# A decoder layer on one core: split weights written by converting and accumulating transfers instead of by ScalarE and VectorE

## The chip, the core and the metric

The kernel runs on one NeuronCore of a Trainium2 chip. The core has TensorE (matmul), VectorE, ScalarE, GpSimd and SyncE, each with its own instruction queue that runs strictly in order, and 16 DMA engines that all queues share. The metric is device time in microseconds (us) of one execution, median of three: 1070.07 us before the change.

## The reference

One layer over 512 tokens of width 1024, in float32: a SwiGLU block (hidden width 2816), a mixer, a second SwiGLU block, a final RMSNorm.

```
h = h + 0.5 * swiglu(rms_norm(h, ffn1_norm), ffn1_w1, ffn1_w3, ffn1_w2)
u = rms_norm(h, mix_norm)
s5_in, q, k, v, r, a_low, g_s5, g_gla = split(u @ w_in)
y_s5  = s5_mixer(s5_in, ...)      # diagonal state space scan, then a GLU
y_gla = gla_mixer(q, k, v, r, a_low, ...)   # chunked gated linear attention
h = h + (sigmoid(g_s5) * (y_s5 @ proj_s5) + sigmoid(g_gla) * (y_gla @ proj_gla)) @ w_out
h = h + 0.5 * swiglu(rms_norm(h, ffn2_norm), ffn2_w1, ffn2_w3, ffn2_w2)
out = rms_norm(h, final_norm)
```

The products need more precision than one pass of the type fp32r gives. So each weight and each activation is written as two fp32r numbers, hi (the rounded value) and lo (what the rounding lost), and each product is three matmuls: hi by hi, hi by lo, lo by hi.

## The kernel before, in words

Work is a list of units. A unit is one weight piece in HBM (128 partitions by 1024 floats, 512 KB; the pieces of ffn1_w2 have 768 or 640 columns) with the matmuls that use it. Most units have 8 k-steps of three matmuls (`mm3`, lines 228 to 230): L228 uses hi of the weights, L229 hi again with lo of the activations, L230 lo of the weights. Units are numbered here from 0 in the order of the list: 0 and 1 are the first pair (`lead1`, which loads x and its own weights in eight small pieces each, interleaved); 2 to 75 are the rest of the first SwiGLU; from 76 the mixer; from 119 `w_out`; from 127 the first six features of the second SwiGLU. Of the units from 2 to 138, 136 go through `load` and `split` in their plain form (104 of 1024 columns, 32 of 768 or 640); the exception is a small one of the mixer, `wal`. After unit 138 the second SwiGLU runs on other code (`ffn_seven`, a seven-product scheme) that fetches from SyncE into the same ring `raws`, and splits on ScalarE and VectorE.

The order is written out by hand, in the loop at lines 1720 to 1739; each engine's queue gets its instructions in just this order. At unit n the loop

- calls `load(n + 5)`: a ring slot is taken and SyncE transfers the piece into `raw`;
- emits the unit's matmuls and releases the slots of unit n - 1;
- calls `split(n + 3)`: ScalarE rounds `raw` into `hi` (L262), VectorE writes `lo = raw - hi` (L263). For a unit marked `urgent` (the last feature of each group of the first SwiGLU: units 11, 31, 49, 67) this comes after the unit's post-processing;
- emits the unit's post-processing (VectorE and ScalarE, for example the gate `silu(a) * b` and its own split);
- lets side generators emit a step: `s5_prep` (preparation of the state space tables, from unit 6 on), later `s5_main` and `gla`.

Rings: 5 slots of `raw`, 4 of `hi`, 4 of `lo`; `get()` gives one of NSLOT = 63 slots of 128x512 floats for everything else. A slot that is taken again makes its new writer wait for the last reader.

What runs on GpSimd before the change: `make_identity` at the start; the first step of `s5_prep`, emitted at unit 6 (three transfers, three memsets of 128x2048, then `wup` and the mask triangle `tri`, L450 to L465, after which VectorE makes `mask` from `tri`, L466); 64 small copies (L608) in four steps of 16, emitted at units 17, 17, 18 and 19; six small transfers (L649); eight tensor operations (L711, L714) emitted at unit 52; memsets of the attention part (L884, L920, L1060, L1077); four multiplications at the end (L1294). None of the weight transfers is on its queue: they are all on SyncE's.

Of the kernel before, what the change touches and what calls it, by code (L numbers as in the profile page):

```python
# [7 lines left out]
F32 = mybir.dt.float32  # L8
F32R = mybir.dt.float32r
I32 = mybir.dt.int32  # L10
U8 = mybir.dt.uint8
AF = mybir.ActivationFunctionType
ALU = mybir.AluOpType
PSUM = bass.MemoryType.PSUM

P = 128
# [4 lines left out]
GROUPS2 = [6, 4, 4, 4, 4]  # L21
BLOCKS = [(0, 256), (256, 384), (384, 512)]
EPS = 1e-6
NSLOT = 63
MAGIC = 12582912.0
HALVES = [slice(0, 256), slice(256, 512)]
STEPS_S5 = [[("a", 0)], [("b", 0)], [("s", 0), ("a", 1)], [], [("b", 1), ("c", 0)], [("s", 1), ("a", 2)], [],
# [45 lines left out]
def body(nc, tc, a):  # L73
    with tc.tile_pool(name="sb", bufs=1) as sb, \
            tc.tile_pool(name="ps", bufs=1, space=PSUM) as pp, \
            tc.manual_schedule():
        _body(nc, a, sb, pp)


def _body(nc, a, sb, pp):  # L80
    V, S, G, PE = nc.vector, nc.scalar, nc.gpsimd, nc.tensor

    def tt(out, x, y, op):
        V.tensor_tensor(out=out, in0=x, in1=y, op=op)  # L84
# [7 lines left out]
    def sub(out, x, y):  # L92
        tt(out, x, y, ALU.subtract)
# [10 lines left out]
    def act(out, x, f, **kw):  # L104
        S.activation(out, x, f, **kw)  # L105

    raws = Ring([sb.tile([P, 1024], F32, name=f"raw{i}") for i in range(5)])
    his = Ring([sb.tile([P, 1024], F32R, name=f"hi{i}") for i in range(4)])
    los = Ring([sb.tile([P, 1024], F32R, name=f"lo{i}") for i in range(4)])
    vec = sb.tile([P, 40], F32, name="vec")  # L110
    s5p = sb.tile([P, 64], F32, name="s5p")
# [12 lines left out]
    def get(dt=F32):  # L124
        made[0] += 1
        return sb.tile([P, T], dt, tag="g", name=f"g{made[0]}", bufs=NSLOT)

# [112 lines left out]
    def load(n):  # L240
        if n >= len(units):
            return
        u = units[n]
        if u.load is not None:
            u.load(u)
        else:
            u.raw = raws.take()
            nc.sync.dma_start(out=u.raw[:, 0:u.width], in_=u.src)

    def split(n):  # L250
        if n >= len(units):
            return
        u = units[n]
        if u.split is not None:
            u.split(u)
            if u.raw is not None:
                raws.drop(u.raw)
                u.raw = None
            return
        u.hi, u.lo = his.take(), los.take()  # L260
        w = u.width
        act(u.hi[:, 0:w], u.raw[:, 0:w], AF.Copy)  # L262
        sub(u.lo[:, 0:w], u.raw[:, 0:w], u.hi[:, 0:w].bitcast(F32))  # L263
        raws.drop(u.raw)
        u.raw = None

    def release(u):
        for ring, t in ((raws, u.raw), (his, u.hi), (los, u.lo)):
# [117 lines left out]
    def lead1(ua, ub, pa, pb):  # L386
# [10 lines left out]
        def mm():  # L397
            for u in (ua, ub):
                u.hi, u.lo = his.take(), los.take()
            pa[0], pb[0] = spps.get(), spps.get()  # L400
            part = lambda k: ((ua, ub)[k // 4], slice(k % 4 * 256, k % 4 * 256 + 256))
            for k in range(KT):
                u, c = part(k)
                nc.sync.dma_start(out=h[k], in_=a["x"][k])
                nc.sync.dma_start(out=u.raw[:, c], in_=a["w0"][k])
            for n in (2, 3, 4):
                load(n)
            st["n1"] = nrm = Norm()
            for k in range(KT):
                hi_lo_scaled(h[k], g1[:, k:k + 1], xs[k][0], xs[k][1])  # L410
                u, c = part(k)
                act(u.hi[:, c], u.raw[:, c], AF.Copy)
                sub(u.lo[:, c], u.raw[:, c], u.hi[:, c].bitcast(F32))
                for bank, o in ((pa[0], c.start), (pb[0], c.start + P)):
                    mm3(bank, u.hi[:, o:o + P], u.lo[:, o:o + P], xs[k][0], xs[k][1], k == 0, k == KT - 1)
            split(2)
            split(3)
            for k in range(KT):
                nrm.square(h[k])
                nrm.gather()  # L420
# [745 lines left out]
    for m in range(KT):  # L1166
        u = Unit(a["wout"][m], 1024, None)
# [171 lines left out]
    def seven_x(norm):  # L1339
# [35 lines left out]
        for k in range(4):  # L1375
            for kk in (k, k + 4):
                xn[kk] = get()
                stt(xn[kk], h[kk], g2[:, kk:kk + 1], b, ALU.mult, ALU.mult)
            low()
            split(xn[k][:, left], X["1"][0][k], X["1"][1][k], -1.0)  # L1380
            split(xn[k + 4][:, left], X["2"][0][k], X["2"][1][k])
            yield
# [333 lines left out]
    tasks.sort(key=lambda t: t[0])  # L1716
    fetches.sort(key=lambda t: t[0])
    load(0)
    load(1)
    for n, u in enumerate(units):  # L1720
        if n >= 2:
# [79 lines left out]
```

## Time and profile before

| | us |
|---|---|
| median of three runs | 1070.07 (1068.56 to 1070.69) |
| profiled execution, its own time | 1068.79 |
| its span, first to last instruction | 1067.1 |
| TensorE busy in the span | 1052.0 |
| VectorE busy | 718.3 |
| ScalarE busy | 437.7 |
| GpSimd busy | 69.1 |

The profiled execution's time is 1.7 us longer than its span. All times in the rows below are microseconds from the start of the span. PE is TensorE's matmuls, PEld its weight loads (which run beside the matmul before), DVE is VectorE, ACT ScalarE, POOL GpSimd, SP SyncE; POOLq and SPq are the queues of the latter two where they issue transfers. A row of the timeline gives start, duration, engine, line, operation, what is written from what, and how many such instructions are merged in it; in square brackets stands the idle time of the engine just before and what ended it. The line of an instruction is often that of a helper (L84 is any `tensor_tensor` of VectorE, L105 any activation of ScalarE). A unit's place in the trace is found by counting weight loads of L228: 8 for each unit of 1024 columns, 6 or 5 for the narrower ones.

### The profile page before, as it was taken

The page shows a single profiled execution, that of the slowest core. Times are in us where ns is not written, and L with a number is a line of the kernel's source. Part 1 is how long each engine was busy: PE and PEld are TensorE (multiplying, and loading weights), DVE is VectorE, ACT ScalarE, POOL GpSimd, SP SyncE. Part 2 cuts the span into 40 slices and gives each one's busy share as a digit, 9 for nine tenths or more (in the row PEclk, how much of TensorE's full clock was granted, in tenths as well). Part 3 has the DMA queues.
Part 4 walks back from the last instruction along what each step waited for, and adds up shares of the span by engine and source line. Part 5 has one row for each costly group of instructions (what it writes and reads, how often), then busy time and mean ns, then how long its engine had stood idle before and what let it go on. Part 6 is the DMA issues. An engine that isn't in the chain of part 4 may idle for free.

```text
span 1067.1 us, 14471 instructions
## 1 busy us (share of the span) xinstructions
PE 1052.0 (99%) x5544; PEld 905.4 (85%) x5544; DVE 718.3 (67%) x1401; ACT 437.7 (41%) x778; POOL 69.1 (6%) x121
## 2 busy tenths in 40 slices
PE   9999999999999999999999999999999999999995
PEld 7888888888888898888878888888899999999995
DVE  6688654797644555687385755557887778777866
ACT  7323254322222433553645233434443444544444
POOL 4002600100400000001000000000000000000002
PEclk9999999999999999999999999999999999999998
DMA  7323223322422332122122222222133233233222
GB/s 259 122 62 134 79 76 102 127 84 62 149 85 62 111 102 79 60 80 79 60 80 80 81 98 99 100 79 89 63 103 103 89 110 106 102 100 109 91 69 79
DMA packets 34388, 101.41 MB, mean 95 GB/s; under 512 B 4096, under 2 KB 5568, under 8 KB 34320
## 3 DMA queue, kind: packets, MB, share of 16 engines
q1 hardware_dynamic: 33408, 99.17, 28.3%
q0 software_dynamic: 480, 0.79, 0.3%
q8 instruction: 43, 0.70, 0.3%
q10 hardware_dynamic: 432, 0.54, 0.1%
q14 instruction: 25, 0.20, 0.1%
HBM read 98.19 MB, written 2.10 MB: 94 GB/s over the span
## 4 chain that ended last, share of the span: by engine, by line
PE 94%; ACT 2%; DVE 2%; DMA 1%; SPq 0%; issue 0%; DVEq 0%; ACTq 0%
PE mm L228 20%; PE mm L230 20%; PE mm L229 20%; PE mm L1529 5%; PE mm L1528 5%; PE mm L1526 5%; PE sp L228 3%; PE sp L229 3%; PE sp L230 3%; ACT g L105 1%; DVE g L84 1%; PE sp L999 1%; PE sp L1001 1%; PE sp L1000 1%; PE mm L1001 1%; PE mm L1000 1%
## 5 line engine op out<-in xcount | busy, mean ns | idle before, releaser
L228 PE MATMUL mm<-g,hi 128*128 128x512 f32 x944 | 374.2, 396 | 0.0
L230 PE MATMUL mm<-g,lo 128*128 128x512 f32 x944 | 369.6, 392 | 0.1
L229 PE MATMUL mm<-g,hi 128*128 128x512 f32 x944 | 369.3, 391 | 0.0
L84 DVE TENSOR_TENSOR lo<-raw,hi 128x1024 fp32r<-128x1024 f32 (+3 forms) x176 | 198.6, 1133 | 131.8 <-ACT hi L105 131.4
L105 ACT ACTIVATE g<-g 128x512 f32<-128x512 f32 (+4 forms) x227 | 130.5, 582 | 339.0 <-DVE g L84 327.2
L105 ACT ACTIVATE hi<-raw 128x1024 fp32r<-128x1024 f32 (+3 forms) x176 | 170.1, 974 | 110.3 <-PE mm L229 63.8
L230 PEld LDWEIGHTS mm<-g,lo 128*128 128x128 f32 x944 | 177.6, 188 | 41.1 <-DVE lo L84 0.6
L84 DVE TENSOR_TENSOR g<-g,g 128x512 fp32r<-128x512 f32 (+7 forms) x342 | 184.6, 558 | 38.6 <-ACT g L105 32.1
L229 PEld LDWEIGHTS mm<-g,hi 128*128 128x128 f32 x944 | 177.9, 188 | 37.2
L228 PEld LDWEIGHTS mm<-g,hi 128*128 128x128 f32 x944 | 177.8, 188 | 37.1
L84 DVE TENSOR_TENSOR g<-mm,g 128x512 f32<-128x512 f32 (+1 forms) x104 | 58.2, 564 | 47.3 <-PE mm L1529 17.2
L228 PE MATMUL sp<-g,g 128*128 128x512 f32 (+1 forms) x176 | 65.6, 373 | 0.0
L229 PE MATMUL sp<-g,g 128*128 128x512 f32 (+1 forms) x176 | 65.4, 372 | 0.0
L230 PE MATMUL sp<-g,g 128*128 128x512 f32 (+1 forms) x176 | 65.0, 369 | 0.0
L84 DVE TENSOR_TENSOR g<-g,mm 128x512 f32<-128x512 f32 (+1 forms) x72 | 44.3, 623 | 19.7 <-PE mm L230 15.3
L105 ACT ACTIVATE g<-mm 128x256 f32<-128x256 f32 (+1 forms) x50 | 19.3, 387 | 90.6 <-PE mm L1529 78.1
L1529 PE MATMUL mm<-b,lo 128*128 128x256 f32 x192 | 53.6, 279 | 0.0
L1529 PE MATMUL mm<-g,lo 128*128 128x256 f32 x192 | 53.6, 279 | 0.0
L1528 PE MATMUL mm<-b,hi 128*128 128x256 f32 x192 | 53.5, 279 | 0.0
L1526 PE MATMUL mm<-b,hi 128*128 128x256 f32 x192 | 53.5, 279 | 0.0
L1528 PE MATMUL mm<-g,hi 128*128 128x256 f32 x192 | 53.5, 279 | 0.0
L1526 PE MATMUL mm<-g,hi 128*128 128x256 f32 x192 | 53.5, 279 | 0.0
(176 smaller groups left out, 1260.0 us busy)
## 6 DMA issues: line engine op xcount, KB each, us to landing
raw<-win SPq DMA_DIRECT2D x24, 512.0 KB, 3.5
raw<-w1b SPq DMA_DIRECT2D x22, 512.0 KB, 3.5
raw<-w3b SPq DMA_DIRECT2D x22, 512.0 KB, 3.5
raw<-w1a SPq DMA_DIRECT2D x21, 512.0 KB, 3.5
raw<-w3a SPq DMA_DIRECT2D x21, 512.0 KB, 3.5
raw<-w2b SPq DMA_DIRECT2D x32, 256.0 KB, 2.7
raw<-w2a SPq DMA_DIRECT2D x16, 384.0 KB, 3.1
raw<-w2a SPq DMA_DIRECT2D x16, 320.0 KB, 2.8
```

The source lines that it names most:

```text
L84: V.tensor_tensor(out=out, in0=x, in1=y, op=op)
L105: S.activation(out, x, f, **kw)
L228: PE.matmul(out, lhsT=wh, rhs=xh, start=start, stop=False)
L229: PE.matmul(out, lhsT=wh, rhs=xl, start=False, stop=False)
L230: PE.matmul(out, lhsT=wl, rhs=xh, start=False, stop=stop)
L999: PE.matmul(banks[i], lhsT=xh, rhs=wh, start=(k == 0), stop=False)
L1000: PE.matmul(banks[i], lhsT=xh, rhs=wl, start=False, stop=False)
L1001: PE.matmul(banks[i], lhsT=xl, rhs=wh, start=False, stop=(k == KT - 1))
L1526: PE.matmul(bank, lhsT=wh[:, c], rhs=xh[k], start=start and k == 0, stop=False, skip_group_check=True)
L1528: PE.matmul(bank, lhsT=wh[:, c], rhs=xl[k], start=False, stop=False, skip_group_check=True)
L1529: PE.matmul(bank, lhsT=wl[:, c], rhs=xh[k], start=False, stop=k == 3, skip_group_check=True)
```

## The change

In `load`, a plain unit's piece no longer goes to `raw` from SyncE. GpSimd issues a transfer with a type conversion, float32 in HBM to fp32r in SBUF, straight into `hi`. In `split`, ScalarE writes `lo = -hi`, and GpSimd issues a second transfer of the same piece from HBM, with an addition at the destination: `lo = -hi + piece`. VectorE's subtraction is gone for these 136 units. Units with their own `split` (`wal`) and the first pair are as before, and so is everything after unit 138. The rings become 4 `raw`, 7 `hi`, 4 `lo`, and NSLOT becomes 59.

```diff
-NSLOT = 63
+NSLOT = 59
...
-    raws = Ring([sb.tile([P, 1024], F32, name=f"raw{i}") for i in range(5)])
-    his = Ring([sb.tile([P, 1024], F32R, name=f"hi{i}") for i in range(4)])
+    raws = Ring([sb.tile([P, 1024], F32, name=f"raw{i}") for i in range(4)])
+    his = Ring([sb.tile([P, 1024], F32R, name=f"hi{i}") for i in range(7)])
...
-            u.raw = raws.take()
-            nc.sync.dma_start(out=u.raw[:, 0:u.width], in_=u.src)
+            if u.split is not None:
+                u.raw = raws.take()
+                nc.sync.dma_start(out=u.raw[:, 0:u.width], in_=u.src)
+                return
+            u.hi = his.take()
+            G.dma_start(out=u.hi[:, 0:u.width], in_=u.src)
...
-        u.hi, u.lo = his.take(), los.take()
+        u.lo = los.take()
         w = u.width
-        act(u.hi[:, 0:w], u.raw[:, 0:w], AF.Copy)
-        sub(u.lo[:, 0:w], u.raw[:, 0:w], u.hi[:, 0:w].bitcast(F32))
-        raws.drop(u.raw)
-        u.raw = None
+        act(u.lo[:, 0:w], u.hi[:, 0:w].bitcast(F32), AF.Copy, scale=-1.0)
+        G.dma_start(out=u.lo[:, 0:w], in_=u.src, accum_op=ALU.add)
```

## Rows read from the trace of the kernel before

**Rows 1.** The page, part 1: busy us (share of the span) xinstructions, by engine.

```profile
PE 1052.0 (99%) x5544; PEld 905.4 (85%) x5544; DVE 718.3 (67%) x1401; ACT 437.7 (41%) x778; POOL 69.1 (6%) x121
```

**Rows 2.** The waits of PE: waiter <- releaser: us in total, times, longest.

```profile
PE sp L904 <- ACT g L105: 2.4, 1, 2.4
```

**Rows 3.** The page, part 5: VectorE's groups that write lo.

```profile
L84 DVE TENSOR_TENSOR lo<-raw,hi 128x1024 fp32r<-128x1024 f32 (+3 forms) x176 | 198.6, 1133 | 131.8 <-ACT hi L105 131.4
```

**Rows 4.** DMA queues (packets, MB, share); issues (KB, median us to landing).

```profile
q1 hardware_dynamic: 33408, 99.17, 28.3%
q0 software_dynamic: 480, 0.79, 0.3%
...
raw<-w1a SPq DMA_DIRECT2D x21, 512.0 KB, 3.5
...
g<-s5bc POOLq DMA_DIRECT2D x2, 256.0 KB, 4.9
```

**Rows 5.** View of the tile raw: its transfers, issue to landing.

```profile
DMA to landing us min/median/max: 2.0/3.4/8.3
```

**Rows 6.** Stretches: length, busy us by engine, granted clock, DMA share, GB/s.

```profile
10.00:15.00 5.00, 5.00 (x20) 3.82 (x21) 4.86 (x10) 4.75 (x10) 1.65 (x5) 1.00 0.99 344
535.00:538.00 3.00, 0.59 (x6) 0.39 (x4) 2.54 (x4) 1.60 (x2) 0.00 (x0) 1.00 0.33 87
539.00:542.50 3.50, 3.50 (x10) 2.75 (x9) 3.08 (x5) 1.72 (x3) 0.00 (x0) 0.52 0.02 5
```

**Rows 7.** The timeline of all engines, the first 20 us.

```profile
10.96 0.33 SPq L248 DMA_DIRECT2D raw<-w1a  x1
...
14.82 0.41 ACT L105 ACTIVATE hi<-raw 128x256 fp32r<-128x256 f32 x1
...
18.16 2.49 DVE L84 TENSOR_TENSOR lo<-raw,hi 128x1024 fp32r<-128x1024 f32 x2 [2.05 <-ACT hi L105]
...
19.44 0.19 PEld L230 LDWEIGHTS mm<-g,lo 128*128 128x128 f32 x1 [0.56 <-DVE lo L84]
```

**Rows 8.** The timeline of POOL.

```profile
1.10 0.29 POOL masks.py:199 TENSOR_SCALAR_AFFINE_SELECT idn<-idn 128x128 f32<-128x128 f32 x1
1.55 0.73 POOL L450 DMA_DIRECT2D s5p<-s5p  x1 [0.16 <-issue]
...
11.64 0.14 POOL L465 MEMSET tri<- 64x64 f32 x1
...
98.57 27.23 POOL L608 COPY g<-g 64x64 f32<-64x64 f32 x64 [54.76 <-DVE g L84]
...
279.17 1.46 POOL L711 TENSOR_TENSOR g<-idn,s5p 128x512 f32<-128x512 f32 x1 [81.99 <-DVE g L84]
...
289.74 2.16 POOL L714 TENSOR_TENSOR b<-b,g 128x512 f32<-128x512 f32 x1
```

**Rows 9.** The timeline of all engines: unit 21 begins its weight loads.

```profile
113.86 0.19 PEld L229 LDWEIGHTS mm<-g,hi 128*128 128x128 f32 x1
...
114.09 0.19 PEld L230 LDWEIGHTS mm<-g,lo 128*128 128x128 f32 x1
```

**Rows 10.** The timeline of all engines, 276 to 289 us.

```profile
276.52 2.46 DVE L84 TENSOR_TENSOR g<-g,g 128x256 f32<-128x256 f32 x6
...
288.45 0.19 PEld L230 LDWEIGHTS mm<-g,lo 128*128 128x128 f32 x1
```

**Rows 11.** The timeline of all engines, behind the urgent unit 49.

```profile
269.87 1.35 ACT L105 ACTIVATE hi<-raw 128x640 fp32r<-128x640 f32 x2
...
274.71 0.19 PEld L230 LDWEIGHTS mm<-g,lo 128*128 128x128 f32 x1
```

**Rows 12.** The timeline of all engines, 73 to 80 us: unit 13.

```profile
73.51 0.83 ACT L105 ACTIVATE hi<-raw 128x768 fp32r<-128x768 f32 x1
...
79.76 0.19 PEld L230 LDWEIGHTS mm<-g,lo 128*128 128x128 f32 x1
```

**Rows 13.** The timeline of DVE, behind unit 6.

```profile
50.89 0.22 DVE L100 TENSOR_SCALAR mask<-tri 128x128 uint8<-128x128 f32 x1
```

## The prediction, made before the result was known

> **What bounds the kernel now.** First the page's busy times: TensorE is busy for 1052.0 of 1067.1 us, VectorE for 718.3, GpSimd for 69.1 [rows 1]. So the reader is to see two things: taking work from VectorE can give back at most the 15 us in which TensorE stands, and GpSimd has room in sum. Then TensorE's waits: only one inside the layer is long, 2.4 us at L904 [rows 2], and behind it the clock is granted at 0.52 (its 1.2 GHz level) over 3.5 us, after a stretch in which TensorE was busy for 0.59 of 3 us [rows 6]. So a stall of some 2 us costs about 1.7 us more (3.5 us at half speed), and I add 1.7 to every such stall below. The rest of the 15 us lies at the start and in the tail, which the change does not relieve. Last, the pace: weight loads follow each other by 0.23 us [rows 9], so a unit of 24 lasts 5.5 us, and any stall is lost for good, since TensorE has no slack to make it up.
>
> **What goes and what costs nothing.** VectorE loses 136 subtractions, some 1.13 us each [rows 3], about 155 us. It is not the bound, so this is worth what stands behind VectorE: the wait at L904 hangs on a chain of ScalarE and VectorE through the attention part in which three subtractions stand. I take the 2.4 us and the 1.7 us behind it as gone: -4.1. What is late next there is TensorE itself. ScalarE writes -hi in place of hi, the same size, priced at nothing. The ring `raws`, 4 for 5, matters after unit 138: the code holds five slots at times there, so a fetch moves later by up to three of its short steps, but it is issued some ten steps ahead and lands in 3.5 us [rows 4]: nothing; without that cover, a few us per group. NSLOT 59 makes slots come round four sooner; TensorE waited for no slot before, so nothing, and a few us in the mixer if that is wrong.
>
> **What is added: a new chain.** In the loop's order, GpSimd's queue at unit n holds: transfer of hi for n+5, second transfer for n+3, then whatever the side generators emit. The second transfer waits for ScalarE's -hi; behind it on GpSimd wait the next hi, the next second transfer and `s5_prep`, and VectorE waits for `s5_prep`. The lo of unit n+3 now lands D after ScalarE, where VectorE took 1.13 us. D is the unknown. No row shows an accumulating transfer. Below: 3.5 us, SyncE's plain 512 KB; GpSimd's own largest, 256 KB, took 4.9 [rows 4]; above: 8.3, the slowest landing of any weight [rows 5]. I take 5.0, nearest to GpSimd's own. Issuing one costs GpSimd 0.7 us [rows 8]. The Trainium skill, "DMA: Bandwidth & Descriptors", section "Anatomy of one DMA — SWDGE (gpsimd) path", gives a GpSimd transfer as 2.0 us plus bytes over 436 GB/s: an estimate of 3.2 us for 512 KB, which is under the 4.9 us that the trace shows for half of that; by it the sum below would be near 1089.
>
> *Start.* Units 2 to 4 were issued from SyncE behind x, at 10.96 us [rows 7]. GpSimd has nothing in front of them but `make_identity`, over at 1.4 us [rows 8], so 1.6 MB join the DMA engines while these are already full: share 0.99 at 344 GB/s [rows 6]. The 0.5 MB that `s5_prep` loaded there move out. Net 1.0 MB at 0.344 MB per us: x comes 2.9 us later. The last ScalarE instruction of the lead ends at 15.2 [rows 7], now 18.1; -hi of unit 2 takes 1.06, so 19.2, plus D is 24.2, where TensorE loaded this lo at 19.44 [rows 7]. Cost 4.8 (2 without the crowding), and 1.7 for the clock.
>
> *First step of `s5_prep`.* It ran at 1.55 to 11.8 us, in front of everything [rows 8]. Now it stands behind the transfers of units 11 and 9, near 50 us, for 10.2 us, and `mask` on VectorE, at 50.89 [rows 13], waits for its end. VectorE gets four subtractions back (4.5), so the gate of unit 9 and ScalarE behind it are 5.7 us later. The -hi of unit 13 ended at 74.3 [rows 12]: 80.0, plus D 85.0. TensorE needs it at 79.76 [rows 12] plus the 6.5 us it is late by now: no stall; if the whole chain moves with TensorE, 5.2. I take 1.5.
>
> *Copies.* 64 copies filled GpSimd from 98.57 for 27.2 us [rows 8], 6.8 us for each step of 16; two steps are emitted at unit 17, then one each at 18 and 19. Counted from TensorE's position, the first two end at 112.2; then come the hi of unit 23 and, 0.7 us later, the second transfer of unit 21, with 1.6 us of another piece in front of it on the DMA engines (0.283 of 1067 us for 99 MB [rows 4] makes 1.6 us for 512 KB). It lands at 119.5; the need was 114.09 [rows 9]: 5.4 us. The next two steps take 6.8 + 1.4 against TensorE's 5.5: 2.7 each. Sum 10.8; VectorE, which feeds the copies, is relieved, so I take 9 (4 to 14), and 1.7 once for the clock.
>
> *Unit 52.* Eight tensor operations hold GpSimd from 279.17 to 291.9 [rows 8], released by VectorE's work that ends at 279.0 [rows 10]. They are emitted ahead of hi 58 and the second transfer of unit 56, which then lands at 291.9 + 0.7 + 1.6 + 5.0 = 299.2; the need was 288.45 [rows 10]: 10.7. VectorE's two subtractions fewer in front: 9 (4 to 13), and 1.7.
>
> *Behind urgent units.* ScalarE finished unit 52's piece at 270.55 (the first of the two merged) and TensorE needed it at 274.71 [rows 11]: 4.2 of slack against D = 5.0, so 0.9, twice (units 49 and 67): 1.8. At D = 8.3 a dozen more units of the first block would stall, some 15 us.
>
> **Sum.** 4.8 + 1.7 + 1.5 + 9 + 1.7 + 9 + 1.7 + 1.8 - 4.1 = 27.1. The profiled execution took 1068.8 us (its span and 1.7 around it), so 1095.9; it lies 1.3 under the median of three, inside their spread. I say 1096.
>
> **Rivals.**
> *GpSimd is never late (1073).* Copies and tensor operations slip between the transfers, for VectorE, relieved, may feed them earlier. Then 4.8 + 1.7 + 1.8 - 4.1 = 4.2. For it: GpSimd is busy for 6% [rows 1]. Against: it is solid for 27 us just where two units a step need it.
>
> *A rate decides (about 1180).* Per unit the DMA engines move the piece twice and read lo as well. At GpSimd's own queue's mean, 0.3% for 0.79 MB [rows 4], 512 KB take 2.1 us; an addition that counts double 4.2; together 6.4 against 5.5 us: 0.9 for each of 126 units' worth (104 + 8 x 22 / 8) is 111 us. At SyncE's rate it would be 1.6 + 3.2 = 4.8, under the pace. The same follows if an issue takes GpSimd 2.8 us, not 0.7. The Trainium skill, "SBUF — State Buffer", section "SBUF: two separate sides", warns of just that: a VectorE instruction that uses both of its ports keeps GpSimd from writing descriptors. The trace's instructions of the kind it names are short (0.22 us for `mask` [rows 13]), so I don't put it in the sum.
>
> *Faster (1065).* One mechanism: the relieved chain at L904 gives 4.1 us, and the new chain stays under the slack everywhere. At the start this needs D = 3.5 and x not delayed: 15.2 + 1.06 + 3.5 = 19.8 against 19.44, 0.4 us. It decides if the copies and unit 52 leave less than 3.7 us. Against: 10 us of GpSimd's work in one piece, twice, in front of transfers whose slot comes free only three units, 16.5 us, before TensorE needs them.
>
> *It does not do what it says.* If the conversion does not round, lo is all zero; instructions, bytes and time are the same, so it has no case of its own.
>
> **Chances.** Forecast 0.60, GpSimd never late 0.14, rate 0.14, faster 0.12. A difference under 0.2% (2.1 us) can't be told from none here. Faster 0.09 (most of the last case), same 0.10 (the rest of it, and half of the 1073 case), slower 0.81. The forecast's own range, with D from 3.5 to 8.3, is 1080 to 1125. For 8 in 10 I reach down to 1070, to take in the 1073 case, and up to 1160, for half of the rate case; outside lie 0.12 below and 0.07 above.
>
> **What would show it.** VectorE's busy time falls to about 560 us and the group of subtractions is left with the 40 of the lead and of `ffn_seven`; q0 carries 66 MB, or 132 if both transfers count there. *Start right:* TensorE's load of unit 2's lo waits for a DMA near 24 us. *GpSimd's order right:* TensorE waits for DMAs into lo at units 21 to 23 and 56, each followed by a stretch at 1.2 GHz, while POOL is solid with copies or tensor operations. *D right:* accumulating transfers land in 4 to 6 us. *Wrong:* TensorE waits for lo in every unit (rate); or no wait for lo outside the start (1073 or 1065); or waits for g slots in the mixer (NSLOT); or the wait at L904 still there.

## The result: 1098.8 us, 2.7% slower, and the profile after

The changed kernel takes 1098.84 us (median; 1096.80 to 1099.88), the kernel before 1069.32 beside it: a ratio of 1.0268 with a 95% interval of 1.0255 to 1.0282. The forecast was 1096. The profiled execution took 1099.1 us, its span is 1097.4, 30.3 more than before.

First the page of the changed kernel: busy us by engine, and the DMA queues (packets, MB, share).

```profile
PE 1062.6 (97%) x5544; PEld 909.6 (83%) x5544; DVE 572.9 (52%) x1265; ACT 437.1 (40%) x778; POOL 251.4 (23%) x393
...
q0 software_dynamic: 39648, 132.93, 52.5%
q1 hardware_dynamic: 13824, 33.10, 9.1%
```

Beside [rows 1] VectorE has lost 145 us and GpSimd gained 182, most of it the issuing of its 272 transfers, which the page counts as busy; beside [rows 4] the bytes have gone from SyncE's queue q1 to GpSimd's q0. TensorE, which bounds the kernel, is busy for 10.6 us more with the same 5544 matmuls: it ran part of them at its lower clock. The other 20 us are waits of TensorE (waiter <- releaser: us, times, longest):

```profile
PE mm L230 <- DMA lo<-w3a: 7.3, 2, 4.8
PE mm L230 <- DMA lo<-w2a: 6.7, 4, 5.3
PE mm L230 <- DMA lo<-w1a: 4.9, 1, 4.9
PE sp L228 <- ACT hi L105: 3.1, 2, 2.1
```

L230 is the third matmul of a k-step, the only one that reads lo. 18.9 us are waits for an accumulating transfer to land; the wait of [rows 2] is no longer in the list. Behind each long wait TensorE ran at 1.2 GHz for a while: the first four of these stretches. The fifth has no wait in front of it (more on it at the end). Stretches of the changed kernel (length; PE, PEld, DVE, ACT, POOL busy; granted clock, DMA share, GB/s):

```profile
25.30:32.10 6.80, 6.18 (x15) 4.83 (x16) 0.00 (x0) 1.06 (x1) 1.23 (x3) 0.50 1.08 290
...
83.30:86.70 3.40, 2.82 (x7) 2.25 (x8) 2.95 (x17) 0.00 (x0) 0.00 (x0) 0.50 1.06 234
...
134.50:141.40 6.90, 6.19 (x15) 4.84 (x16) 0.00 (x0) 1.89 (x4) 6.05 (x22) 0.51 0.78 179
...
318.80:322.30 3.50, 3.30 (x8) 2.62 (x9) 0.00 (x0) 1.06 (x1) 1.22 (x3) 0.51 1.13 311
...
431.50:434.90 3.40, 3.40 (x10) 2.72 (x9) 1.60 (x10) 0.00 (x0) 0.00 (x0) 0.50 0.23 45
```

So each stall cost more than its own length: 3.4 to 3.5 us at half speed followed it at units 11 and 56, 6.8 to 6.9 at units 2 and 21, which lose some 1.7 and 3.4 us.

**Where the 30.3 us stand.** The start of every unit in the trace after, less its start in the trace before, is a staircase; each step is a loss that TensorE never makes up. The steps are rounded one by one, their sum is not.

| step | forecast, us | measured, us |
|---|---|---|
| start: x late, lo of unit 2, clock behind it | 6.5 | 9.4 (1.7 + 7.7) |
| first step of `s5_prep` (units 9 to 11) | 1.5 | 5.7 |
| copies (unit 21), clock | 10.7 | 7.9 |
| tensor operations (unit 56), clock | 10.7 | 7.1 |
| behind urgent units | 1.8 | 2.6 |
| units 76 and 79, just ahead of and in the mixer | 0 | 1.9 |
| wait at L904, clock | -4.1 | -4.6 |
| steps too small to name | | 0.4 |
| sum | 27.1 | 30.3 |

The start, from the timeline of all engines of the changed kernel:

```profile
16.74 1.99 ACT L105 ACTIVATE lo<-hi 128x1024 fp32r<-128x1024 f32 x2
...
18.08 0.88 POOL L267 DMA_DIRECT2D lo<-w1a  x1 [14.76 <-ACT lo L105]
...
25.92 0.29 PEld L230 LDWEIGHTS mm<-g,lo 128*128 128x128 f32 x1 [5.38 <-DMA lo<-w1a]
```

ScalarE's -hi of unit 2 (the first of two merged) ends at 17.8; GpSimd, which had waited 14.8 us for it, issues the second transfer; lo is there 7.8 us later, where VectorE took 1.13 [rows 3].

The first step of `s5_prep`, unit 11 (the timeline of all engines):

```profile
60.45 5.66 POOL L459 MEMSET b<- 128x2048 f32 x3
...
68.94 0.23 DVE L100 TENSOR_SCALAR mask<-tri 128x128 uint8<-128x128 f32 x1 [11.17 <-POOL tri L467]
...
75.10 0.63 ACT L105 ACTIVATE g<-g 128x512 f32<-128x512 f32 x1 [16.16 <-DVE g L84]
...
78.37 0.86 POOL L267 DMA_DIRECT2D lo<-w3a  x1 [7.33 <-ACT lo L105]
...
83.88 0.80 PE L230 MATMUL mm<-g,lo 128*128 128x512 f32 x1 [2.51 <-DMA lo<-w3a]
```

Read the brackets upwards: TensorE waits for the DMA, the DMA was issued late because GpSimd waited for ScalarE, ScalarE for VectorE, VectorE 11.2 us for GpSimd's own memsets. The ring closes on GpSimd.

The copies, unit 21 (POOL, then TensorE):

```profile
114.58 12.10 POOL L610 COPY g<-g 64x64 f32<-64x64 f32 x32
...
127.16 0.90 POOL L267 DMA_DIRECT2D lo<-w3a  x1
...
135.21 0.79 PE L230 MATMUL mm<-g,lo 128*128 128x512 f32 x1 [4.76 <-DMA lo<-w3a]
```

and the tensor operations, unit 56:

```profile
311.15 1.29 POOL L716 TENSOR_TENSOR b<-b,g 128x512 f32<-128x512 f32 x1
...
312.97 0.90 POOL L267 DMA_DIRECT2D lo<-w2a  x1
...
319.00 0.80 PE L230 MATMUL mm<-g,lo 128*128 128x512 f32 x1 [5.26 <-DMA lo<-w2a]
```

In both the second transfer is issued 0.5 us after the end of GpSimd's own work, and TensorE's wait is what the transfer then takes, 8.1 and 6.0 us, less what slack was left.

### The profile page after: what moved, and what is told of

Its sections match the earlier page's. It is cut to its first block, busy times and chain, and to the rows that moved or that the text cites. A ratio compares the mean times of both kernels' runs of the same rounds, so it can differ in the third digit from the quotient of the medians.

```text
span 1097.4 us, 14401 instructions
## 1 busy us (share of the span) xinstructions
PE 1062.6 (97%) x5544; PEld 909.6 (83%) x5544; DVE 572.9 (52%) x1265; ACT 437.1 (40%) x778; POOL 251.4 (23%) x393
## 2 busy tenths in 40 slices
DMA packets 53971, 167.47 MB, mean 153 GB/s; under 512 B 6272, under 2 KB 7744, under 8 KB 53904
## 3 DMA queue, kind: packets, MB, share of 16 engines
q0 software_dynamic: 39648, 132.93, 52.5%
## 4 chain that ended last, share of the span: by engine, by line
PE 86%; DMA 4%; POOL 3%; DVE 3%; ACT 1%; issue 1%; SPq 0%; DVEq 0%; ACTq 0%; POOLq 0%
PE mm L230 18%; PE mm L228 18%; PE mm L229 17%; PE mm L1531 5%; PE mm L1530 5%; PE mm L1528 5%; PE sp L228 3%; PE sp L229 3%; PE sp L230 3%; DVE g L84 2%; DMA lo<-w2a 2%; POOL g L610 1%; ACT g L105 1%; PE sp L1002 1%; PE sp L1001 1%
## 5 line engine op out<-in xcount | busy, mean ns | idle before, releaser
L230 PE MATMUL mm<-g,lo 128*128 128x512 f32 x944 | 374.1, 396 | 19.0 <-DMA lo<-w3a 7.3
L230 PEld LDWEIGHTS mm<-g,lo 128*128 128x128 f32 x944 | 179.4, 190 | 63.7 <-DMA lo<-w2a 9.6
L105 ACT ACTIVATE lo<-hi 128x1024 fp32r<-128x1024 f32 (+2 forms) x136 | 133.9, 990 | 141.9 <-PE mm L230 94.5
L1296 POOL TENSOR_TENSOR g<-g,g 128x512 f32<-128x512 f32 x4 | 5.4, 1369 | 290.8 <-ACT g L105 290.8
L230 PE MATMUL sp<-g,g 128*128 128x512 f32 (+1 forms) x176 | 65.0, 369 | 0.0
L96 DVE SCALAR_TENSOR_TENSOR g<-mm,g 128x512 f32<-128x512 f32 x27 | 18.6, 690 | 80.2 <-PE mm L230 80.1
L1528 PE MATMUL mm<-g,hi 128*128 128x256 f32 x192 | 53.5, 279 | 0.0
```

Source lines behind the costliest of these rows:

```text
L96: V.scalar_tensor_tensor(out=out, in0=x, scalar=s, in1=y, op0=op0, op1=op1)
L230: PE.matmul(out, lhsT=wl, rhs=xh, start=False, stop=stop)
L1528: PE.matmul(bank, lhsT=wh[:, c], rhs=xh[k], start=start and k == 0, stop=False, skip_group_check=True)
```

## The experiments

Theory: lo now comes by a way that is 6 to 8 us long instead of 1.1, through a queue that runs in order and also holds GpSimd's own work; it is late where that work, or a late ScalarE, stands in front of it. Rivals: the shorter rings cost the time; the rate of GpSimd or of the DMA engines does; the converting transfers alone do. In each, "step" is a step of the staircase.

**The rings alone.** The kernel before with `NSLOT = 59`, 4 `raw`, 7 `hi`; unit 4 is loaded behind the lead, as 4 slots of `raw` ask.

> The kernel before with the ring sizes of the change alone (4 raw, 7 hi, 4 lo, 59 slots); unit 4 is loaded after the lead instead of within it, since 4 raw slots allow no more. If the ring sizes cost nothing, as the prediction had it: 1069.3 us, within 2. If the fewer slots cost in the mixer or behind unit 138: 1072 or more, with new waits of TensorE there.

1069.77 us, ratio 0.9995 (0.9986 to 1.0004). The rings cost nothing.

**Units 2 and 3 as before.** In the changed kernel, `load` and `split` of these two take the old way:

```diff
-            if u.split is not None:
+            if u.split is not None or u in plain:    # plain = units 2 and 3
```

> The changed kernel, but units 2 and 3 are loaded from SyncE behind x and split by ScalarE and VectorE as before. The changed kernel is 9.35 us behind at unit 3 (1.67 in the lead, the rest a wait for lo of unit 2 and 6.8 us at 1.2 GHz). Theory: both come from the two early pieces and the late lo, so about 9 us go: 1090. Rival (the lag would be made elsewhere, since what GpSimd and VectorE do at units 11, 21 and 56 waits for them and not for TensorE): less than 4 us go, 1095 or more.

1088.4 us, ratio 1.0174 (1.0156 to 1.0193): 10.4 us less than the changed kernel. The 7.7 us of unit 2's lo are gone (x's 1.7 to 2.1 stay), and units 21 and 56 still stall, by steps of 5.4 and 5.7. The preparation still costs 5.8, in four small steps at units 9 to 13.

**GpSimd clear of its own work.** The first step of `s5_prep` goes behind the first three transfers, ahead of everything else; copies, memsets and tensor operations go to VectorE:

```diff
+            next(prep)
             st["n1"] = nrm = Norm()
...
-                        G.tensor_copy(xv[half, :, gg, 3 - j, :], ...)
+                        V.tensor_copy(xv[half, :, gg, 3 - j, :], ...)
...
-            G.tensor_tensor(out=mm_, in0=mm_, in1=w0, op=ALU.add)
+            V.tensor_tensor(out=mm_, in0=mm_, in1=w0, op=ALU.add)
```

> The changed kernel, but GpSimd's other work is out of the transfers' way: the first step of the table preparation is issued during the lead (behind the first three hi transfers), and the 64 copies, 8 memsets and 8 tensor operations are on VectorE. Theory (GpSimd's order makes the waits at units 11, 21 and 56): these three go, 5.9 + 7.9 + 7.1 us: 1078. Rival (the transfers' own rate or landing time makes them; the DMA engines are busy for 61% now): the waits stay or move to neighbouring units, 1090 or more.

1085.82 us, ratio 1.0147 (1.0130 to 1.0163). The steps at units 9 to 11, 21 and 56 are gone, 20.6 us, as the theory has it (the start, at 10.5, is 1.1 longer). But one of 7.7 us came up at unit 24 (timeline of ACT and POOL):

```profile
137.56 0.42 ACT L105 ACTIVATE b<-g 64x256 f32<-64x256 f32 x1 [17.41 <-DVE g L84]
...
139.99 1.06 ACT L105 ACTIVATE lo<-hi 128x1024 fp32r<-128x1024 f32 x1
...
141.35 0.86 POOL L267 DMA_DIRECT2D lo<-w1a  x1 [19.48 <-ACT lo L105]
```

VectorE now does the copies, ScalarE waits 17.4 us for it, and -hi stands behind that wait. It is the same mechanism one engine up: whatever holds ScalarE holds lo.

**Both.** Units 2 and 3 as before, and GpSimd clear.

> GpSimd's copies, memsets and tensor operations moved to VectorE as in the run with a clear GpSimd, and units 2 and 3 loaded and split as before the change. Theory (the causes add): the start's 10.5 us shrink to about 2, while the stall at unit 24 (ScalarE 17 us behind VectorE) stays at 7.7: 1076 to 1079. Rival (the stall at unit 24 came from the late start, since VectorE's work and TensorE's stood differently by it): without it, 1069 to 1072.

1077.05 us, ratio 1.0071 (1.0058 to 1.0084), as the theory expected: the two causes nearly add (13.0 and 10.4 us apart, 21.8 together), and the step at unit 24 (7.8) did not come from the start.

**From the mixer on only.** Units 2 to 75 as before, the change from unit 76 on; unit 4 is loaded behind the lead.

> The change from unit 76 (the mixer) on alone; the first block's units are loaded and split as before. Theory: all stalls but 2 us of units 77 and 80 belong to the first block, and the 4.6 us that the changed kernel gains in the attention part stay: between 1064.7 and 1067 us, faster than before. Rival (that gain came because the whole attention chain stood later or because the DMA transfers crowd each other here too): 1069 or more.

1064.73 us, ratio 0.9955 (0.9942 to 0.9967): faster than before. All of TensorE's waits of 0.6 us or more:

```profile
PE mm L1287 <- DVE g L84: 2.4, 1, 2.4
PE mm L155 <- DVE stat L96: 2.2, 1, 2.2
PE sp L394 <- DVE idle L391: 1.2, 1, 1.2
PE sp L228 <- ACT hi L105: 0.6, 1, 0.6
```

None is for lo, and none stands at the place of [rows 2]. So the loss comes from the change in the first SwiGLU, and the gain from the change in the mixer. (The 1.9 us that the changed kernel loses at units 76 and 79 do not show here.)

**The converting transfer alone.** hi by GpSimd's transfer, raw by SyncE's, the subtraction on VectorE (5 `raw`, 7 `hi`, NSLOT 57):

```diff
-        act(u.lo[:, 0:w], u.hi[:, 0:w].bitcast(F32), AF.Copy, scale=-1.0)
-        G.dma_start(out=u.lo[:, 0:w], in_=u.src, accum_op=ALU.add)
+        sub(u.lo[:, 0:w], u.raw[:, 0:w], u.hi[:, 0:w].bitcast(F32))
```

> The first half of the change alone: GpSimd's converting transfer writes hi, and SyncE's transfer of the same piece still writes raw, from which VectorE subtracts hi as before the change (5 raw, 7 hi, NSLOT 57). No accumulating transfer, no -hi on ScalarE. Theory (it is the accumulating transfer, whose landing stands between ScalarE and TensorE, that stalls; the transfer of hi has two more units of slack): x is 1.7 us later at the start, nothing at units 21 and 56, the wait at L904 stays: 1070 to 1073. Rival (any weight transfer in GpSimd's queue behind its copies is late): stalls at units 23 to 25 and near 58, 1080 or more.

1072.59 us, ratio 1.0032 (1.0021 to 1.0042). In the first block nothing but the start, 4.0 us; the weights of units 21 to 25 and 56 are in time. (1.5 us at unit 79 and 2.3 at the start of unit 104 come to it; on the latter see the slots below.) The wait at L904 did not stay, against what I had expected: -4.6 here too, with all subtractions on VectorE (716.5 us busy). So that the time lies in the expected range is in part luck: the start cost 4.0 and not 1.7, the steps at 79 and 104 were not foreseen, and the gain at L904 made up for them. Why the wait went, the timelines show, first of VectorE, ScalarE and TensorE in the kernel before, then the same subtraction (the 106th of the trace) in this run:

```profile
534.51 1.22 DVE L84 TENSOR_TENSOR lo<-raw,hi 128x1024 fp32r<-128x1024 f32 x1 [1.65 <-ACT hi L105]
...
536.37 0.63 ACT L105 ACTIVATE g<-g 128x512 f32<-128x512 f32 x1 [1.89 <-DVE g L84]
536.91 1.06 ACT L105 ACTIVATE g<-sp 128x512 f32<-128x512 f32 x1
...
538.02 1.16 PE L904 MATMUL sp<-g,g 64*128 64x128 f32 x8 [2.43 <-ACT g L105]
```

```profile
532.48 1.22 DVE L84 TENSOR_TENSOR lo<-raw,hi 128x1024 fp32r<-128x1024 f32 x1
```

The subtraction had stood 1.65 us waiting for ScalarE's rounding, with the chain to L904 behind it: ScalarE waits for VectorE, TensorE for ScalarE. In this run it waits for nothing and comes 2.0 us sooner, though TensorE is 5.5 us behind by then. Taking the rounding off ScalarE ends the wait as well as taking the subtraction off VectorE does; the next run shows the latter by itself (-4.3 at L904, with one more pass on ScalarE). The landing of hi in this run, and in the changed kernel (min/median/max):

```profile
DMA to landing us min/median/max: 3.1/4.0/11.5
```

```profile
DMA to landing us min/median/max: 3.5/6.8/11.8
```

The two kernels move the same bytes (167.48 and 167.47 MB), but here 48.9% of the DMA engines' time is taken, there 61.6%. So beside accumulating transfers, in the same queue, the converting ones took 2.8 us longer.

**The accumulating transfer alone.** raw and hi as before, and then

```diff
-        sub(u.lo[:, 0:w], u.raw[:, 0:w], u.hi[:, 0:w].bitcast(F32))
+        act(u.lo[:, 0:w], u.raw[:, 0:w], AF.Copy, scale=-1.0)
+        G.dma_start(out=u.lo[:, 0:w], in_=u.src, accum_op=ALU.add)
```

> The second half of the change alone: SyncE loads raw and ScalarE rounds it into hi as before the change (rings and NSLOT as before), then ScalarE writes lo = -raw, rounded, and GpSimd's accumulating transfer adds the piece. GpSimd's queue holds no transfer of hi. Theory 1 (the accumulating transfer alone carries the stalls: its landing, 6 us, and GpSimd's own work in front of it): x is not delayed, but unit 2 still waits about 5 us for lo and 1.7 to 3.4 behind it at 1.2 GHz; units 21 and 56 stall as in the changed kernel, 7 each; 1090 to 1097. Theory 2 (the stalls come from the loop in GpSimd's queue, where the next transfer of hi stands behind a second transfer that waits for the landing of an earlier hi): without hi there GpSimd reaches its copies and tensor operations earlier, the stalls at 21 and 56 shrink by half or go: 1075 to 1085.

1110.32 us, ratio 1.0383 (1.0359 to 1.0407), outside both theories. TensorE's waits:

```profile
PE mm L230 <- DMA lo<-w2a: 11.0, 3, 4.3
PE mm L230 <- DMA lo<-w1a: 8.7, 1, 8.7
PE mm L230 <- DMA lo<-w3a: 8.4, 2, 4.6
```

Units 11 and 21 stall (6.9 and 6.8) without any hi in GpSimd's queue, so the loop of theory 2 isn't needed for that; unit 56 does not: the tensor operations began 5.7 us later than in the changed kernel, but TensorE was 12 us later by then. What neither foresaw: lo lands in 7.6 us here, raw of `w1a` and `w3a` in 7.1 (3.5 in [rows 4]), ScalarE does two passes over each piece, and so the units behind urgent ones stall (14, 52 and 70: steps of 4.9, 6.2, 4.0). The issues of that raw (KB, median us to landing):

```profile
raw<-w1a SPq DMA_DIRECT2D x21, 512.0 KB, 7.1
```

So the accumulation, with one more pass on ScalarE in this form, carries the whole loss and more; what each of the two would cost by itself was not measured.

**The split one unit sooner.** In the first SwiGLU -hi and the second transfer are emitted for n+4 instead of n+3 (5 `lo`, NSLOT 57).

```diff
-            split(n + 3)
+            ahead(n)        # split(n + 4), up to unit 75
```

> The changed kernel, but in the first SwiGLU -hi and the second transfer are emitted one unit sooner (for unit n+4 instead of n+3; 5 slots of lo instead of 4, NSLOT 57 instead of 59). Theory (lo is late because the second transfer is asked too late for its way through GpSimd's queue; it is a matter of slack, not of throughput): one unit is 5.5 us, the stalls at units 11, 21 and 56 were 2.5, 4.8 and 5.3 us, all shorter, so they go with their stretches at 1.2 GHz: -4.2 - 7.9 - 7.1 = -19.1, and the 2.8 us behind urgent units go too. The start (9.4) stays. 1077 to 1080. Rival 1 (GpSimd or its DMA queue has no throughput to spare around the copies): the stalls come back one unit later, time within 3 us of 1099. Rival 2 (ScalarE now stands waiting for hi to land, as it did at unit 24 of the run with a clear GpSimd, and VectorE's chain behind it is late): new stalls, 1090 or more.

1096.55 us, ratio 1.0252 (1.0238 to 1.0265): the theory's number fails, and the numbers of both rivals hold. Unit 11's stall went (4.2 to 0.7), but units 22 and 57 stall in place of 21 and 56, by steps of 6.6 and 7.8: one unit later, as rival 1 has it. (3.7 us more stand at the start of unit 104; on these see the slots below.) ScalarE in front of the copies:

```profile
103.63 0.84 ACT L105 ACTIVATE lo<-hi 128x768 fp32r<-128x768 f32 x1 [3.50 <-DMA hi<-w2a]
107.02 0.85 ACT L105 ACTIVATE lo<-hi 128x768 fp32r<-128x768 f32 x1 [2.54 <-DMA hi<-w2a]
111.17 1.06 ACT L105 ACTIVATE lo<-hi 128x1024 fp32r<-128x1024 f32 x1 [3.31 <-DMA hi<-w1a]
```

-hi waits for hi to land, each time; GpSimd waits for -hi, and the next hi stands behind it. Over units 17 to 21 a second transfer was issued 6.8 to 8.4 us before its use, in the changed kernel 8.1 to 11.3: emitted sooner, it came out later. That is the wait of rival 2; whether throughput is short as well, as rival 1 says, the run after the next tells.

**The same with units 2 and 3 as before.**

> As the run with the split one unit sooner, and units 2 and 3 loaded by SyncE and split on ScalarE and VectorE as before the change. Theory (the causes add): the start's stall of 7.7 us and its half clock go as well, and what is left is 1.7 us for x, 1 to 3 for the table preparation, 1.5 for the clock at unit 80, -4.6 in the mixer: 1069 to 1073, no difference from before. Rival (relief in one place moves the stall to the next unit, as the run with units 2 and 3 alone showed in part, -10.4 for 13.2 of causes): 1076 or more.

1090.97 us, ratio 1.0191 (1.0175 to 1.0207): the rival. The start's 7.7 us are gone, units 21, 22 and 57 stall by 2.1, 7.8 and 7.5; 3.7 us at unit 104 come from the slots here too.

**hi one unit sooner too.** `load(n + 6)`, 8 `hi`, 5 `lo`, NSLOT 55.

> As the run with the split one unit sooner, and the transfer of hi one unit sooner too (for n+6 instead of n+5), in the first SwiGLU: 8 slots of hi, 5 of lo, NSLOT 55. Theory (the split one unit sooner gained little because -hi then waited 6 to 7 us for hi to land and held GpSimd's queue: the whole chain must move, not its last link): the stalls at units 22 and 57 of that run, 6.6 + 0.8 and 7.8, go; the start stays; 3 to 5 us near unit 104 from NSLOT, since 57 already showed 3.7 there: 1079 to 1084. Rival (work of GpSimd in one piece stalls whatever stands behind it, at any lead): stalls of 5 to 8 us twice more, 1092 or more.

1095.20 us, ratio 1.0250 (1.0231 to 1.0270). The number is the rival's, but the theory is borne out in part: units 22 and 23 lose 0.7 and 1.0 where it was 6.6 and 0.8, unit 57 4.2 where it was 7.8. So at unit 22 it was not throughput that was short. What hides this is a step of 7.0 at the start of unit 104, in the mixer, and 3.3 behind unit 138.

**The slots alone.** The kernel before with `NSLOT = 55`.

> The kernel before with NSLOT 55 instead of 63 and nothing else changed: weights as before, by SyncE, ScalarE and VectorE. The four runs with NSLOT 57 or 55 each lost 2 to 7 us at unit 104 of the mixer, those with 59 or 63 nothing. Theory (the slots alone do it: the loop comes round eight slots sooner and a writer waits for a reader): a step of 3 to 7 us at unit 104, 1072 to 1077. Rival (it takes the shorter ring together with GpSimd's transfers in the mixer): no step there, 1069 to 1071.

1083.03 us, ratio 1.0129 (1.0109 to 1.0148): steps of 1.5 and 8.0 at the starts of units 103 and 104, and 3.8 us more behind unit 138. TensorE's waits there are for ScalarE (first line; the second is the wait of [rows 2], unchanged); which slot makes ScalarE late was not traced:

```profile
PE mm L228 <- ACT g L105: 3.4, 3, 1.6
PE sp L904 <- ACT g L105: 2.5, 1, 2.5
```

So eight slots cost 14 us by themselves, more than expected; 59 cost none. Less the 7 to 14 us of the slots, the run before this one stands near 1081 to 1088; what of it is unit 57's stall was not tried apart.

**hi alone, from the mixer on.** The converting transfer and VectorE's subtraction for units from 76 on, the first SwiGLU as before.

> From the mixer on (unit 76) only: hi by GpSimd's converting transfer, raw by SyncE and the subtraction on VectorE; nothing accumulating; the first SwiGLU as before the change. Theory (the wait at L904 hung on VectorE standing for ScalarE's rounding, so relief of either engine ends it; the hi run showed -4.6 there): 1064 to 1066, the same as the run that has the whole change from unit 76 on. Rival (VectorE's subtractions count in the mixer): 1067 or more.

1066.04 us, ratio 0.9965 (0.9952 to 0.9978), 0.04 us above the range that was expected and short of the rival's; the mixer gives -4.6, a stretch at 1.2 GHz in unit 79 takes 1.2 back. Beside 1064.73 the whole change in the mixer has no clear lead: the intervals overlap.

## Why the prediction was right, and where it was off

- **The bound.** TensorE is still the bound; relief of VectorE (145 us, said 155) gave nothing outside one wait. Right.
- **D.** Taken as 5.0. The landings of lo from issue (0.3 us behind ScalarE's end where GpSimd is free), min/median/max:

```profile
DMA to landing us min/median/max: 4.3/6.0/11.7
```

  The four that decided took 7.8, 5.5, 8.1 and 6.0 us: D was too small by 0.5 to 3.1 us, and all four lie inside its bounds of 3.5 and 8.3 (the longest of all, 11.7, does not). The Trainium skill, "DMA: Bandwidth & Descriptors", section "Anatomy of one DMA — SWDGE (gpsimd) path", gave an estimate of 3.2 us for such a piece; no group of 512 KB pieces has so short a median here (3.8 to 5.5 with hi alone, 5.4 to 7.8 in the changed kernel), so the measurement decides.
- **Start.** The mechanism as forecast. x was 1.7 us late, not 2.9; D 7.8, not 5.0; the half clock 6.8 us long, not 3.5.
- **First step of `s5_prep`.** The term that was mis-sized: 1.5 taken, 5.7 measured. The prediction named the case (5.2 if the whole chain moves with TensorE) and gave it too little weight; the rows at 60 to 84 us show that it did move, and the stall came at unit 11, not 13.
- **Copies.** 7.9 for 10.7. Unit 21's wait came out as worked out (4.8 for 5.4), but in part by luck: counted from TensorE's position its second transfer went out 1.7 us sooner and then took 8.1 us where 6.6 were worked out; and the half clock behind it lasted 6.9 us, not 3.5. Units 22 and 23 did not stall: the 64 copies took 12.1 + 5.1 + 4.5 = 21.7 us, not 27.2 as in [rows 8], and TensorE was at half clock meanwhile. That the copies are the cause, the run with GpSimd clear shows.
- **Unit 52.** 7.1 for 10.7. The eight operations began about 1 us sooner, counted from TensorE's position, and took 9.5 us (302.9 to 312.4), not 12.7 [rows 8].
- **Behind urgent units.** 2.6 for 1.8, in steps of 0.3 to 0.9 at units 14, 52, 53 and 70: behind three of the four urgent units, not two. (The slack of 4.2 leaves 0.8 against a D of 5.0, not 0.9.)
- **L904.** -4.6 for -4.1. Size right, reason half right: VectorE's standing for ScalarE was in the chain as well as the subtraction, and with that wait gone the subtraction itself does no harm, as the run with hi alone shows.
- **Rings.** NSLOT 59 costs nothing, as said; the warning of "a few us in the mixer" came true at 57 and 55.
- **Rate.** Not the bound. The queue's time (52.5% of 1097 us) has room, and the changed kernel from the mixer on loses nothing. But the transfers fill enough of the DMA engines to lengthen each other's landings: while the four transfers that decided were on their way, 83, 75, 70 and 88% of the engines' time was taken. The Trainium skill, "SBUF — State Buffer", section "SBUF: two separate sides", would have GpSimd's issues held up while VectorE runs an instruction that uses both of its ports; the 272 issues took 0.87 us on average and 1.27 at the longest, none near the 2.8 at which that rival begins, so this trace shows no such hold-up. (With hi alone, VectorE being busy for 716.5 us, the 136 issues took 0.53.)
- **What was missed.** 1.5 us at unit 79: TensorE fell to 1.2 GHz (431.5 in the stretches above) with no wait in front of it. Why it fell stays open: a step of 1.2 to 1.5 us stands there in eight of the fourteen traces of this case, in the other six none.

The sum came within 3.2 us of the measured shift because two terms too small (start and first step, 7.1 together) met two too large (copies and unit 52, 6.4). The mechanism was right, save that the prediction leaned to no stall at the table preparation; that the number came so near is in part luck.

## What to carry to other kernels

An engine with spare time in sum is no free place for a step on the critical path: the step takes the length of its new way, and stands behind everything that the new queue holds in order. Before moving a step, write down the new queue in order and ask of each long item which transfer stands behind it; and ask the same of the engine that releases it. Where one part of a kernel has the slack and another not, make the change there alone: here that turned +2.7% into -0.45%.

## What was not expected of the hardware

- Accumulating transfers fill the DMA engines for longer than their bytes say. Packets of 4096 bytes took a median of 174 ns on q0 in the run with hi alone, 328 ns in the run with the accumulating transfer alone, and 159 ns on SyncE's q1 in both. By queue share a piece of 512 KB takes 1.7 us of the DMA engines when it is converted (20.6% of 1070 us, the run with hi alone, over 126 units' worth) and 2.9 when it is accumulated (33.5% of 1107 us, the run with the accumulating transfer alone); both are estimates.
- GpSimd's own instructions got faster where VectorE has no subtractions: the copies went from a mean of 380 ns to 295, L711's operations from 1293 to 1042, L714's from 1847 to 1295. Other runs agree: with subtractions in the first SwiGLU the copies took 366 to 381 ns (hi alone, with GpSimd's transfers, 366), without them 279 to 297 (the accumulating transfer alone 296). By what way VectorE slows them was not traced. The copies in the groups of POOL (busy us, mean ns, then idle), before and after:

```profile
L608 POOL COPY g<-g 64x64 f32<-64x64 f32 x64 | 24.3, 380 | 57.6 <-DVE g L84 54.8
```

```profile
L610 POOL COPY g<-g 64x64 f32<-64x64 f32 x64 | 18.9, 295 | 2.9
```

- The clock fell once with no wait of TensorE in front of it. In the changed kernel 16 matmuls of one column each, with two others, filled 2.8 us at full clock, and 0.7 us later the clock was 0.50; in the kernel before, the same part of the code kept 1.00 (stretches of both, columns as above):

```profile
428.00:430.80 2.80, 2.80 (x18) 2.77 (x16) 0.00 (x0) 0.00 (x0) 0.00 (x0) 1.00 1.02 342
```

```profile
394.80:397.40 2.60, 2.60 (x16) 2.60 (x16) 0.00 (x0) 0.00 (x0) 0.00 (x0) 1.00 0.00 0
397.50:401.00 3.50, 3.50 (x15) 3.50 (x16) 2.10 (x13) 0.00 (x0) 0.00 (x0) 1.00 0.04 7
```
